# Tiles 61 and 62 stored each in its own transfer instead of together: the last stores of a matmul with bias and residual

## The chip, the cores and the metric

One core of one Trainium2 chip. The metric is the device time of one execution in microseconds (us), as a median of several. Engines: PE is TensorE, DVE is VectorE, ACT is ScalarE, POOL is GpSimd, SP is the engine that issues all transfers. "The 16 engines" below are the core's DMA engines.

## The reference

```python
def setup_inputs():
    batch, m, k, n = 16, 512, 1024, 768      # x, weight, bias, residual, all float32
    ...
def reference(x, weight, bias, residual):
    return (np.matmul(x, weight) + bias + residual).astype(np.float32)
```

That is 8192 rows in 64 tiles of 128 rows by 768 columns. In and out together are 87 MB.

## The kernel before

Sixteen tiles make a group; in the output, 16 rows of one partition lie next to each other, so a store of several tiles is 128 rows of (tiles x 3072) bytes. SP issues loads ("x", "r", "w", "b") and stores ("s" for whole tiles, "c" for a column piece of the last one) strictly in the order of one list. An entry goes out when all that it needs is done:

```python
ORDER = [ ... cut ...
 ('r', 3, 7, 16), ('s', 2, 0, 16), ('s', 3, 0, 10), ('s', 3, 10, 13),
 ('s', 3, 13, 15), ('c', 3, 15, 0), ('c', 3, 15, 1)]
OUTSIDE = 4
LAST = [(0, 512), (512, 256)]

    def pump():
        while queue:
            kind, S, j0, j1, *cut = queue[0]
            ... cut ...
            else:
                need = [("out", J * S + j) for j in range(j0, j1)]
            if not all(n in done for n in need):
                return
            queue.pop(0)
```

So ('s', 3, 13, 15) stores tiles 61 and 62 once both are done. Tile 63 is computed and stored in two column pieces, of 512 and 256 columns. The end of the program waits for the landing of the stores: all but the last four, then a barrier, then the last four.

```python
    with tc.tile_critical():
        landed = prog.emit(stores)
        for sem, value in landed[:-OUTSIDE]:
            nc.sync.wait_ge(sem, value)
    with tc.tile_critical(sync_engine=mybir.EngineType.SP):
        for sem, value in reversed(landed[-OUTSIDE:]):
            nc.sync.wait_ge(sem, value)
```

Of the kernel before, what the change touches and what calls it, by code (L numbers as in the profile page):

```python
# [32 lines left out]
 ('r', 1, 6, 16), ('s', 0, 0, 16), ('x', 2, 0, 6), ('r', 2, 0, 6), ('x', 2, 6, 16),  # L33
 ('r', 2, 6, 16), ('s', 1, 0, 16), ('x', 3, 0, 6), ('r', 3, 0, 7), ('x', 3, 6, 16),
 ('r', 3, 7, 16), ('s', 2, 0, 16), ('s', 3, 0, 10), ('s', 3, 10, 13),
 ('s', 3, 13, 15), ('c', 3, 15, 0), ('c', 3, 15, 1)]
OUTSIDE = 4
LAST = [(0, 512), (512, 256)]

# [368 lines left out]
```

## Time and profile before

| | before |
|---|---|
| time, median of 3 runs | 210.03 us (209.96 to 210.3) |
| span of the profiled run | 208.5 us |
| TensorE busy | 97% |
| DMA engines busy on the main queue | 97.9% |
| result of tile 61 / of tile 62 there | 200.53 / 202.61 us |
| last result there | 204.60 us |
| last piece landed | 207.27 us |

The lines are in the prediction. Three views matter: the timeline of the end (when a result is there), the issues with their time to landing (when a store is complete), and the half-microsecond stretches, whose second last column is the mean busy share of the 16 DMA engines. A share of 0.5 does not say whether each engine is half busy or half of them are idle. The records of single increments and packets in the trace do: each store raises its semaphore 16 times, once for each DMA engine. Times told below as "first increment" and "last increment" are from these records, as are packet times.

Two more stretches of before, which the result will be held against (start and end, then busy time of PE, PEld, DVE, ACT, POOL, the granted clock, the DMA share, GB/s):

```profile
204.50:205.00 0.50, 0.00 (x0) 0.00 (x0) 0.10 (x1) 0.00 (x0) 0.00 (x0) 1.00 0.99 393
206.00:206.50 0.50, 0.00 (x0) 0.00 (x0) 0.00 (x0) 0.00 (x0) 0.00 (x0) 1.00 0.90 318
```

Most engines are busy until 206.5; then only the last one still works (its last packet ends at 206.93).

### The profile page before, as it was taken

Reading aid. Unit: us, or ns where it says so; the run is one execution under the profiler, and the core shown is the slowest. Engines: PE = TensorE matmul, PEld = TensorE weight load, DVE = VectorE, ACT = ScalarE, POOL = GpSimd, SP = SyncE. Lnnn points to the kernel's source line nnn. Section 1 sums busy time; section 2 is a strip of 40 time slices with the busy share of each in tenths; the row PEclk is TensorE's granted clock in tenths of the full one; section 3 lists DMA queues with packets and bytes.
Section 4 is the critical chain, followed back from the end, with each engine's and each line's share of the span. In section 5 each row is a group of like instructions: output and inputs, shape, how many; then the busy total and the mean of one; then the engine's idle time right before and its main releaser. Section 6 shows DMA issues by size and latency. Waiting matters only on the chain.

```text
span 208.5 us, 2492 instructions
## 1 busy us (share of the span) xinstructions
PE 201.6 (97%) x1298; PEld 80.8 (39%) x794; DVE 105.3 (51%) x141; ACT 66.1 (32%) x69; POOL 115.2 (55%) x71
## 2 busy tenths in 40 slices
PE   7899999999999999999999999999999999999991
PEld 2333434443443444344334434433443443344340
DVE  1457555445545543654554454555445545544542
ACT  2444522402640282420280094230092047430000
POOL 1100029859999904999029801999207960899200
PEclk9999999999999999999999999999999999999998
DMA  5999999899999999999998999999999999999985
GB/s 216 425 425 445 426 423 475 385 427 425 485 409 416 449 395 438 453 396 437 410 493 387 432 445 429 443 443 385 423 450 468 416 398 471 415 443 417 427 351 232
DMA packets 4627, 87.20 MB, mean 418 GB/s; under 512 B 516, under 2 KB 644, under 8 KB 1416
## 3 DMA queue, kind: packets, MB, share of 16 engines
q1 hardware_dynamic: 4616, 87.05, 97.9%
q8 instruction: 8, 0.13, 0.2%
q14 instruction: 3, 0.02, 0.0%
HBM read 61.88 MB, written 25.17 MB: 417 GB/s over the span
## 4 chain that ended last, share of the span: by engine, by line
PE 92%; DMA 4%; DVE 1%; SPq 0%; ACT 0%; issue 0%
PE psum_o L257 79%; PE pt L250 13%; DMA x_tile<-in_x_dram 4%; SPq L168 0%; DVE xt L226 0%; ACT xb L226 0%; DVE ro L229 0%; SPq L403 0%; SPq L371 0%
## 5 line engine op out<-in xcount | busy, mean ns | idle before, releaser
L257 PE MATMUL psum_o<-w_sb,xt 128*128 128x256 bf16 (+1 forms) x1024 | 176.6, 326 | 0.5 <-DVE xt L226 0.5
L229 POOL TENSOR_TENSOR ro<-ro,bias_sb 128x768 f32<-128x768 f32 x50 | 88.8, 1817 | 46.9 <-DMA ro<-in_residual_dram 46.9
L226 ACT CAST xb<-x_tile 128x1024 bf16<-128x1024 f32 (+1 forms) x63 | 61.3, 1023 | 117.1 <-DMA x_tile<-in_x_dram 88.6
L268 PEld LDWEIGHTS <-xt 128*128 128x128 bf16 x520 | 50.9, 98 | 102.9 <-issue 101.0
L226 DVE COPY xt<-pt 128x1024 bf16<-128x1024 bf16 x64 | 44.1, 691 | 83.4 <-PE pt L250 83.4
L229 DVE TENSOR_TENSOR ro<-psum_o,ro 128x768 f32<-128x768 f32 (+2 forms) x51 | 47.6, 934 | 6.5 <-POOL ro L229 4.5
L250 PE MATMUL pt<-ident,xb 128*128 128x128 f32 x256 | 38.3, 274 | 0.6 <-DVE xb L226 0.4
L229 POOL TENSOR_TENSOR ro<-ro 128x768 f32<-128x768 f32 x14 | 24.9, 1818 | 25.0 <-DMA ro<-in_residual_dram 24.9
L250 PEld LDWEIGHTS pt<-ident,xb 128*128 128x128 f32 x256 | 29.7, 141 | 15.6 <-issue 12.3
L229 DVE TENSOR_TENSOR ro<-psum_o,bias_sb 128x768 f32<-128x768 f32 x14 | 13.2, 948 | 0.0
L312 PE MATMUL psum_o<-warm 128*128 128x512 bf16 x18 | 6.3, 506 | 1.4 <-DVE warm_a L232 1.4
L226 DVE CAST xb<-x_tile 128x512 bf16<-128x512 f32 (+1 forms) x4 | 1.9, 492 | 6.2 <-DMA x_tile<-in_x_dram 6.2
L226 ACT CAST w_sb<-ro 128x768 bf16<-128x768 f32 x4 | 3.3, 832 | 3.7 <-DMA ro<-in_weight_dram 3.7
L226 POOL CAST w_sb<-ro 128x768 bf16<-128x768 f32 x1 | 0.8, 822 | 6.0 <-DMA ro<-in_weight_dram 6.0
L312 PEld LDWEIGHTS psum_o<-warm 128*128 128x128 bf16 x18 | 2.1, 124 | 4.5 <-issue 2.7
L226 DVE CAST w_sb<-ro 128x768 bf16<-128x768 f32 x3 | 1.7, 557 | 2.0 <-DMA ro<-in_weight_dram 2.0
L226 ACT ACT_TABLE_LOAD x1 | 1.3, 1283 | 0.9 <-SPq L371 0.9
L329 DVE STREAM_SHUFFLE bias_sb<-bias_row 128x768 f32<-128x768 f32 x1 | 1.0, 1007 | 0.0
L232 DVE MEMSET warm<- 128x256 uint32 x1 | 0.3, 272 | 1.1 <-SPq L371 1.1
L232 DVE MEMSET bias_row<- 128x768 f32 x1 | 0.7, 698 | 0.2 <-issue 0.2
L232 POOL MEMSET ident<- 128x128 f32 x1 | 0.2, 204 | 0.5 <-SPq L371 0.5
L320 POOL TENSOR_SCALAR_AFFINE_SELECT ident<-ident 128x128 f32<-128x128 f32 x1 | 0.3, 292 | 0.2 <-POOL ident L232 0.2
(7 smaller groups left out, 0.7 us busy)
## 6 DMA issues: line engine op xcount, KB each, us to landing
out_dram<-ro SPq DMA_DIRECT2D x3, 6144.0 KB, 34.6
x_tile<-in_x_dram SPq DMA_DIRECT2D x3, 5120.0 KB, 24.5
ro<-in_residual_dram SPq DMA_DIRECT2D x3, 3840.0 KB, 32.4
x_tile<-in_x_dram SPq DMA_DIRECT2D x3, 3072.0 KB, 34.0
ro<-in_residual_dram SPq DMA_DIRECT2D x3, 2304.0 KB, 18.7
x_tile<-in_x_dram SPq DMA_DIRECT2D x4, 1024.0 KB, 10.9
x_tile<-in_x_dram SPq DMA_DIRECT2D x2, 2048.0 KB, 23.4
out_dram<-ro SPq DMA_DIRECT2D x1, 3840.0 KB, 13.3
```

Of the source, the lines that this page charges most:

```text
L226: op(eng, lambda e: (e.copy if eng == "act" else e.tensor_copy)(out=dst, in_=src), rd, wr)
L229: op(eng, lambda e: e.tensor_add(out=dst, in0=a, in1=b), rd, wr)
L232: op(eng, lambda e: e.memset(dst, v), [], [wr])
L250: op("pe", lambda e, q=q: e.transpose(out=pt[:, q, :], in_=words[:, ts(q, P)], identity=ident), [("XB", t % XB_N, 2 * q // n_q), "ident"], ...
L257: return e.add_instruction(mybir.InstMatmult(name=nc.get_next_instruction_name(), ins=[e.lower_ap(rhs), e.lower_ap(lhsT, for_matmul_weight ...
L268: op("pe", lambda g: g.ldweights(lhsT), rd)
L312: op("pe", lambda e: e.matmul(PO[i][:, 0:512], lhsT=warm[:, 0:P], rhs=warm, start=True, stop=True), ["warm"], [("PO", i)])
L320: op("pool", lambda e: e.affine_select(out=ident, in_=ident, compare_op=mybir.AluOpType.not_equal, fill=1.0, base=0, pattern=[[-1, P]], ch ...
L329: op("dve", lambda e: e.stream_shuffle(out=bias_sb, in_=bias_row, mask=[0] * QUAD), ["bias_row"], ["bias"])
```

## The change

The intent: tile 61 is done two microseconds before tile 62 and need not wait for it.

```diff
- ('s', 3, 13, 15), ('c', 3, 15, 0), ('c', 3, 15, 1)]
+ ('s', 3, 13, 14), ('s', 3, 14, 15), ('c', 3, 15, 0), ('c', 3, 15, 1)]
```

OUTSIDE stays 4, so the store of tiles 58 to 60 is now waited for ahead of the barrier.

## The prediction

> **What bounds the kernel now.** I read the page first (busy shares, slices, chain), then the timeline and the waits of the last ten microseconds, because the change touches only one of the last stores.
>
> The page, parts 1, 2 and 4:
> ```profile
> span 208.5 us, 2492 instructions
> PE 201.6 (97%) x1298; PEld 80.8 (39%) x794; DVE 105.3 (51%) x141; ACT 66.1 (32%) x69; POOL 115.2 (55%) x71
> ...
> DMA  5999999899999999999998999999999999999985
> ...
> q1 hardware_dynamic: 4616, 87.05, 97.9%
> ...
> PE 92%; DMA 4%; DVE 1%; SPq 0%; ACT 0%; issue 0%
> ```
> Two things run flat out side by side: TensorE, busy 97% of the span, and the DMA engines, 97.9% of 16 engines' time on one queue. No stage up to the last few microseconds is touched, so all that can be won or lost lies after the last matmul, and in how far the stores are behind it there. The timeline of the end, columns start, duration, engine and instruction, with the idle time before it in brackets:
> ```profile
> 196.55 0.95 DVE L229 TENSOR_TENSOR ro<-psum_o,ro 128x768 f32<-128x768 f32 x1
> 199.58 0.95 DVE L229 TENSOR_TENSOR ro<-psum_o,ro 128x768 f32<-128x768 f32 x1
> 201.65 0.96 DVE L229 TENSOR_TENSOR ro<-psum_o,ro 128x768 f32<-128x768 f32 x1 [1.11 <-PE psum_o L257]
> 203.30 0.69 DVE L229 TENSOR_TENSOR ro<-psum_o,ro 128x512 f32<-128x512 f32 x1 [0.70 <-PE psum_o L257]
> 204.18 0.42 DVE L229 TENSOR_TENSOR ro<-psum_o,ro 128x256 f32<-128x256 f32 x1 [0.18 <-PE psum_o L257]
> ```
> These are the results of tiles 60, 61 and 62 and the two column pieces of tile 63. Tile 61 is complete at 199.58 + 0.95 = 200.53, but its store goes with tile 62 and leaves only at 201.65 + 0.96 = 202.61. The last result is there at 204.60, 3.9 us before the span ends. What SP waits for from 204 us on, and the issues of the last stores with their time to landing (one line each for tiles 58 to 60, for 61 with 62, and for the last piece):
> ```profile
> SPq L403 <- DMA out_dram<-ro: 1.4, 3, 0.6
> ```
> ```profile
> out_dram<-ro SPq DMA_DIRECT2D x1, 1152.0 KB, 6.9
> out_dram<-ro SPq DMA_DIRECT2D x1, 768.0 KB, 3.7
> out_dram<-ro SPq DMA_DIRECT2D x1, 128.0 KB, 2.6
> ```
> The landings follow: 197.52 + 6.9 = 204.4; 202.63 + 3.7 = 206.3; 204.63 + 2.6 = 207.2. So the kernel ends with the landing of the last 128 KB at about 207.3 and 1.2 us of closing barriers. The question is whether that landing is late because its data came late or because the DMA engines still had older stores to move. Stretches of half a microsecond (columns: engines' busy time, then granted clock, DMA share, GB/s):
> ```profile
> 201.50:202.00 0.50, 0.50 (x4) 0.20 (x2) 0.35 (x1) 0.00 (x0) 0.00 (x0) 1.00 0.92 387
> 202.00:202.50 0.50, 0.50 (x4) 0.24 (x3) 0.50 (x1) 0.00 (x0) 0.00 (x0) 1.00 0.74 313
> 202.50:203.00 0.50, 0.50 (x4) 0.25 (x3) 0.10 (x1) 0.00 (x0) 0.00 (x0) 1.00 0.61 258
> 203.00:203.50 0.50, 0.50 (x6) 0.36 (x4) 0.20 (x1) 0.00 (x0) 0.00 (x0) 1.00 0.53 221
> 203.50:204.00 0.50, 0.50 (x6) 0.32 (x4) 0.49 (x1) 0.00 (x0) 0.00 (x0) 1.00 0.96 399
> ```
> The dip from 202.0 to 203.5 is real idle time, and it is what the change aims at. It adds up to (0.26 + 0.39 + 0.47) x 0.5 = 0.56 us of all 16 engines, but it is a mean: about half of them stand still, and the others do not. The trace's packet records and the increments of each store's semaphore, one per engine, show which. The 16 increments for tiles 58 to 60 come at 202.13, 202.25, 202.36, 202.47, 203.04, 203.05, 203.44, then 203.76 to 204.19, and the last at 204.44; a packet ends about 0.35 us before its increment, so the engines run out of older work between 201.8 and 204.09. The packets of tiles 61 and 62 begin at 203.47, 0.84 us after their issue. The last engine has no gap: its 9216-byte packets end at 204.08, its eight 6144-byte ones at 205.93, its eight of 2048 at 206.58, its eight of 1024 at 206.93, and its increment is the last one, at 207.27. For every store after 200 us the last increment is 0.24 to 0.30 us behind the fifteenth. The end is the end of this one engine's work.
>
> **What the Trainium skill says.** "Perfetto Trace Analysis", DMA Optimizations, says that splitting may let some chunks start sooner, and helps if DMA engines are generally idle; here they are 97.9% busy and only partly idle for 1.5 us. "DMA: Bandwidth & Descriptors", Queues, rings and completion order: on each engine descriptors are consumed in ring order. The trace agrees: an engine's packets for tile 61 stand behind its own for 58 to 60, whatever time they are issued. The same page, "Why a DMA increments its semaphore by 16 and not by 1": only the full count means that all has landed, so the slowest engine decides; the 16 separate increments above agree. The same page, Bandwidth, advises transfers of 1 MiB and more; here packets cost, by size, 46 ns (1024 B), 84 (2048), 121 (3072, the bias load), 234 (6144) and 347 (9216), some 8 ns plus 0.037 ns a byte, so halving a 768 KB store costs little.
>
> **The change part by part.** Instruction order on TensorE, VectorE, ScalarE and GpSimd is the same; only SP's list changes.
> 1. Removed: one store of 128 rows of 6144 B, issued at 202.63. Added: one of tile 61, 128 rows of 3072 B, issued at about 200.54, and one of tile 62, the same size, still at 202.63. Tile 61's 384 KB become available to the engines 2.09 us earlier.
> 2. SP: one more issue of about 0.33 us (the five stores' issues take 332 to 344 ns each). It falls at 200.54 to 200.87, when SP would be waiting for tile 62. Off the path: 0.
> 3. Engines: each moves 8 packets of 3072 B twice in place of 8 of 6144. Per engine 16 x 121 - 8 x 234 = 1936 - 1872 = +64 ns, and one more semaphore write of 9 ns: +0.07 us.
> 4. Engines that are early (about ten: increments up to 203.83, so packets done by about 203.5): tile 61's packets fill their gap. With first packets possible at 200.54 + 0.84 = 201.4, an engine free at 201.8 does them until 202.8, waits for tile 62 at 203.47, ends it at 204.45, and then waits for the two pieces of tile 63 (204.02 and 204.63 plus 0.84 = 204.86 and 205.47): ends near 205.9 instead of 206.5. That is a gain of 0.6 us for it, and worth nothing for the count of 16.
> 5. The last engine: 204.08 + 16 x 0.121 + 0.01 = 206.03 instead of 205.93; the last piece ends at 206.93 + 0.07 to 0.10 = about 207.0. No gap to fill, so no gain; loss 0.07 to 0.10 us.
> 6. The waits at the end: the program waits for the last four stores after a barrier and for the others before it. With one store more, the store of tiles 58 to 60 is no longer among the last four and moves to the waits before the barrier. It lands at 204.44; SP reaches these waits at 205.0. One more check there, some 0.05 us, is hidden, as SP then waits for stores until 207.3 anyway.
> Sum: +0.07 us on the path, of which I take back 0.05 because with these ten engines done earlier the last may run its packets slightly faster. 210.03 + 0.02 = 210.05.
>
> **The rivals.**
> First: the gap is filled and the end comes earlier. For it: the dip in the DMA share, tile 61 waiting 2.1 us for nothing, and 3.9 us of tail after the last result. The most it could give: the last piece, issued at 204.63, would on free engines need 0.84 + 0.37 + 0.35 = 1.56 us and land at 206.2, so about 1.0 us; limited by the one tile that is moved, 8 x 0.121 = 0.97. Against it: the gap must be on the last engine, and there is none. If in other executions the last engine is less late, so that it too waits for 203.47, part of it could come: perhaps 209.5.
> Second: the shorter packets and the extra store cost more than their fit, for example a gap between stores on each engine of 0.1 to 0.2 us. Against it: in the records an engine goes from 6144-byte to 2048-byte packets with some 10 ns between. It would make 210.2.
> Third: the earlier writes of tile 61 get in the way of the older store on the late engines, or move which engine is last. Reordering among engines can shift the last by the 0.24 to 0.30 us between fifteenth and sixteenth, either way: 209.8 to 210.3.
>
> **Range and chances.** The three runs before spread over 0.34 us (209.96 to 210.3), more than my net effect. Runs on another chip can add as much again. I put the time at 210.05, eight times in ten between 209.5 and 210.5; the lower end holds half of the first rival's 1.0 us. A change of 2% is 4.2 us; the whole tail after the last result is 3.9 us and the moved tile is worth 0.97, so faster by 2% is out of reach (0.004), and nothing added comes near 4.2 us (0.006). Within 2%: 0.99.
>
> **What would show it.** Right: the DMA share from 201.5 to 203.5 rises to near full; a 384 KB store issued near 200.5; SP waits at the end as long as before (1.4 us in three pieces, a few hundredths apart); the last increment again near 207.3, with the early engines' increments for the last piece now down to about 206.3, so a wider spread among the 16; packets of 3072 B at 121 ns. Wrong: last increment by 206.8 or earlier with the span down to 208.0, which would mean that the last engine's lateness is not its own backlog, or 3072-byte writes well over 121 ns.

## The result

| | before | the change |
|---|---|---|
| median, 6 runs each | 210.00 us (209.96 to 210.38) | 210.18 us (210.09 to 210.35) |
| ratio | | 1.0005, 95% interval 0.9992 to 1.0017 |

A ratio is the mean time of one kernel's runs over that of the other's of the same rounds, so not quite the ratio of the medians. The same, within what can be resolved (0.12% of 210 us is 0.25 us).

The page of the changed kernel, the parts that were shown of before:

```profile
span 208.4 us, 2468 instructions
PE 200.3 (96%) x1273; PEld 80.9 (39%) x794; DVE 105.3 (51%) x141; ACT 66.1 (32%) x69; POOL 115.2 (55%) x71
...
DMA  6999999999999999999999999999999999999995
...
q1 hardware_dynamic: 4760, 87.05, 97.9%
...
PE 92%; DMA 4%; issue 1%; DVE 1%; SPq 0%; ACT 0%
```

The span is the same and the same chain bounds it. The 25 missing PE instructions are matmul records missing from the trace (the main matmul's group counts 999 where before has 1024), not work saved. The queue has 144 packets more: 128 more of data, and 16 semaphore writes for one more store.

The timeline of the end (VectorE), the issues with their landing, and SP's waits after 204 us:

```profile
199.79 0.95 DVE L229 TENSOR_TENSOR ro<-psum_o,ro 128x768 f32<-128x768 f32 x1
201.85 0.96 DVE L229 TENSOR_TENSOR ro<-psum_o,ro 128x768 f32<-128x768 f32 x1 [1.11 <-PE psum_o L257]
```
```profile
out_dram<-ro SPq DMA_DIRECT2D x1, 1152.0 KB, 6.6
out_dram<-ro SPq DMA_DIRECT2D x1, 384.0 KB, 4.5
out_dram<-ro SPq DMA_DIRECT2D x1, 128.0 KB, 2.4
```
```profile
SPq L403 <- DMA out_dram<-ro: 1.1, 3, 0.6
```

In this profiled run all results came 0.2 us later than in that of before (tile 61 at 200.74 in place of 200.53). Tile 61's store of 384 KB did leave at once, at 200.76, and landed at 205.28. The last piece was issued at 204.83 in place of 204.63, yet it landed at 207.20, where before has 207.27. That is why SP waits 1.1 us in place of 1.4: it comes later, and what it waits for comes at the same time. A landing that does not follow its issue has something else ahead of it.

The stretches, the five of before and the two added above:

```profile
201.50:202.00 0.50, 0.50 (x4) 0.27 (x3) 0.15 (x1) 0.00 (x0) 0.00 (x0) 1.00 0.97 406
202.00:202.50 0.50, 0.50 (x4) 0.25 (x3) 0.50 (x1) 0.00 (x0) 0.00 (x0) 1.00 1.02 424
202.50:203.00 0.50, 0.50 (x4) 0.24 (x3) 0.31 (x1) 0.00 (x0) 0.00 (x0) 1.00 0.79 332
203.00:203.50 0.50, 0.50 (x5) 0.28 (x3) 0.00 (x0) 0.00 (x0) 0.00 (x0) 1.00 0.62 252
203.50:204.00 0.50, 0.50 (x7) 0.44 (x6) 0.42 (x1) 0.00 (x0) 0.00 (x0) 1.00 0.92 369
...
204.50:205.00 0.50, 0.00 (x0) 0.00 (x0) 0.30 (x1) 0.00 (x0) 0.00 (x0) 1.00 0.68 270
206.00:206.50 0.50, 0.00 (x0) 0.00 (x0) 0.00 (x0) 0.00 (x0) 0.00 (x0) 1.00 0.55 193
```

The gap that the change aimed at is partly filled: 0.97 and 1.02 from 201.5 to 202.5, where before has 0.92 and 0.74 (1.02 is not more than all: the share adds up recorded durations, and neighbouring records overlap a little, see experiment 7). But what was taken there comes back as new idle time: 0.68 from 204.5 (before: 0.99) and 0.55 from 206.0 (before: 0.90). Most engines are now ahead and wait for the pieces of tile 63, and at the very end for one another. The increments of the last piece say it in numbers: the middle one of the 16 came at 206.83 before and at 206.58 now; the last one at 207.27 and 207.20. The many gained 0.25 us, the one that counts nothing that can be told from chance.

### The profile page after: what moved, and what is told of

The parts are those of the page before. It is cut to its first block, busy times and chain, and to the rows that moved or that the text cites. A ratio compares the mean times of both kernels' runs of the same rounds, so it can differ in the third digit from the quotient of the medians.

```text
span 208.4 us, 2468 instructions
## 1 busy us (share of the span) xinstructions
PE 200.3 (96%) x1273; PEld 80.9 (39%) x794; DVE 105.3 (51%) x141; ACT 66.1 (32%) x69; POOL 115.2 (55%) x71
## 4 chain that ended last, share of the span: by engine, by line
PE 92%; DMA 4%; issue 1%; DVE 1%; SPq 0%; ACT 0%
PE psum_o L257 79%; PE pt L250 13%; DMA x_tile<-in_x_dram 4%; SPq L168 0%; DVE xt L226 0%; ACT xb L226 0%; DVE ro L229 0%; SPq L403 0%; SPq L371 0%
```

## The experiments

Theory A, from the prediction: the end is the end of the last DMA engine's work. That engine has no gap, so a tile offered to it earlier waits behind its older packets. Rivals: C, the last piece's own way from issue to landing sets the end; D, idle time of the engines counts as its mean; E, the moved wait costs something.

**1. The change again.** No edit; the same kernel once more, with the repeat of run 2 and with run 3.

> The change itself once more, on the same chip as the next two runs, so that they can be compared. Theory A: +0.0 to +0.1 us against the kernel before; ratio 1.000 within 0.001.

Measured: 210.06 us (209.93 to 210.33, 5 runs), before 210.05 us (11 runs); ratio 1.0001 (0.9989 to 1.0013). As theory A expects. Two occasions now agree on "no difference above some 0.3 us".

**2. Is the moved wait a cost?** Five waits after the barrier put the store of tiles 58 to 60 back where it was.

```diff
- OUTSIDE = 4
+ OUTSIDE = 5
```

> The change with the store of tiles 58 to 60 put back among the waits after the barrier (five in place of four). Theory A: that wait is hidden either way, so the same as the change within 0.05 us (210.1), last increment and span unchanged. If the moved wait cost the change something, this is up to 0.1 us faster than the change.

Measured: 209.98 us (4 runs), before 210.21 us (10 runs); ratio 0.9989 (0.9975 to 1.0003). That was lower than expected, and the interval just reaches 1, so it was repeated in one call with the change and with run 3:

> The change with five waits after the barrier, once more. The first time it was 0.23 us under the kernel before, 0.3 us under what the change showed on another occasion. Theory A (the moved wait is hidden, the difference was chance in how late the last DMA engine is): same as the change of this call within 0.1 us. Rival E (the moved wait costs): 0.2 to 0.3 us faster than the change again.

Measured: 210.15 us (209.8 to 210.5, 5 runs); ratio 1.0007 (0.9994 to 1.0019), now 0.09 us slower than the change. The first result did not come again. The trace of the change agrees: SP is through the waits ahead of the barrier at 205.31, and the last piece lands at 207.20.

**3. The moved wait alone**, on the kernel before:

```diff
- OUTSIDE = 4
+ OUTSIDE = 3
```

> The kernel before with three waits in place of four after the barrier: the moved wait alone, without splitting the store. Theory A: the same as before within 0.1 us. Rival E: +0.2 to +0.3 us.

Measured: 210.2 us (6 runs, 209.96 to 210.24 but for one of 211.53); ratio 1.0013 (0.9994 to 1.0033). The interval alone would leave room for rival E; it is widened by the one odd run, without which the mean is 210.13. Rival E asked for 0.2 to 0.3 us; neither the repeat of run 2 nor this run shows it. A cost of less than some 0.2 us would not be seen.

These runs also give the plainest evidence for theory A. Last increments in us, each from one profiled run:

| run | tiles 58 to 60 | last piece | difference |
|---|---|---|---|
| before | 204.44 | 207.27 | 2.83 |
| before, three waits | 204.47 | 207.22 | 2.75 |
| the change | 204.38 | 207.20 | 2.82 |
| the change again | 204.11 | 206.91 | 2.80 |
| the change, five waits | 204.10 | 206.89 | 2.79 |
| the same again | 203.93 | 206.76 | 2.83 |

Joint or split, the last piece lands 2.75 to 2.83 us after the last engine is through with tiles 58 to 60. That moment itself wanders by half a microsecond from run to run, and it is set before the store in question moves a byte: the last increment of the store of tiles 48 to 57, which is alike in all six, came at 201.69, 201.72, 201.64, 201.38, 201.37 and 201.19 in the same order. The last packet of that store ended at 201.33 at the latest, and the first packet of a split tile 61 began at 201.61 at the earliest. The last engine is not always alone: at the last piece the sixteenth increment is 0.30 and 0.29 us behind the fifteenth in before and in the change, but only 0.00 to 0.06 in the other four runs, where at least two engines share the end.

**4. No backlog: the change where it can help.** Tiles 58 to 60 are not stored at all (a wrong result), so that no engine has older work when tile 61 is done. First with tiles 61 and 62 together:

```diff
- ('s', 3, 0, 10), ('s', 3, 10, 13), ('s', 3, 13, 15),
+ ('s', 3, 0, 10), ('s', 3, 13, 15),
```

> Wrong result on purpose: tiles 58 to 60 are never stored, so no engine has older work when tile 62 is ready; tiles 61 and 62 stored together. Theory A: all engines start them at 203.47, end the last piece at 206.4, last increment 206.75 in place of 207.27: -0.5 us against the kernel before. Serves as the base of the next run. Rival C: 0.

Then with the two apart:

```diff
- ('s', 3, 0, 10), ('s', 3, 10, 13), ('s', 3, 13, 15),
+ ('s', 3, 0, 10), ('s', 3, 13, 14), ('s', 3, 14, 15),
```

> Wrong result on purpose, as the run before it, with tiles 61 and 62 stored singly: the change under test without backlog. Theory A: tile 61 goes from 201.4, tile 62 from 203.47 to 204.45, the pieces of 63 end at 205.9, last increment near 206.25: -0.5 us against the joint form without backlog, -1.0 against the kernel before. If the change does nothing by nature (rival C, the last piece's own way decides): no difference between the two.

Measured: together 209.95 us (209.87 to 210.08, 5 runs), ratio to before 0.9985 (0.9972 to 0.9999); apart 209.44 us (209.41 to 209.96, 5 runs), ratio 0.9964 (0.995 to 0.9978). The same edit that gives nothing in the kernel gives 0.51 us here. The stretches, together and then apart:

```profile
202.00:202.50 0.50, 0.50 (x4) 0.25 (x3) 0.50 (x1) 0.00 (x0) 0.00 (x0) 1.00 0.00 0
202.50:203.00 0.50, 0.50 (x4) 0.20 (x2) 0.25 (x1) 0.00 (x0) 0.00 (x0) 1.00 0.00 0
203.00:203.50 0.50, 0.50 (x5) 0.32 (x4) 0.05 (x1) 0.00 (x0) 0.00 (x0) 1.00 0.00 0
```
```profile
202.00:202.50 0.50, 0.50 (x5) 0.20 (x3) 0.38 (x1) 0.00 (x0) 0.00 (x0) 1.00 1.03 412
202.50:203.00 0.50, 0.50 (x4) 0.26 (x3) 0.50 (x1) 0.00 (x0) 0.00 (x0) 1.00 0.66 258
203.00:203.50 0.50, 0.50 (x4) 0.22 (x3) 0.07 (x1) 0.00 (x0) 0.00 (x0) 1.00 0.00 0
```

Here a share of 0.00 does mean that all 16 engines stand still, and tile 61's packets fill the hole. Two things were off. Against before, the joint form gained 0.26 us in place of 0.5, and the split form 0.77 in place of 1.0; experiment 6 tells why. The difference of the two came out as expected because both fell short by the same quarter of a microsecond. And the profiled run of the split form was its slowest (209.96; the other four lie between 209.41 and 209.60): its last piece was issued at 205.10, 0.32 later than in the joint run's profile, and landed at 206.94, 1.84 us after its issue. With the backlog gone, the end followed the last result in that run, so that a late result was a late end.

**5. Tile 61 taken off the engines.** The change without its new store (a wrong result):

```diff
- ('s', 3, 13, 14), ('s', 3, 14, 15),
+ ('s', 3, 14, 15),
```

> Wrong result on purpose: the change with tile 61 never stored, so its 0.97 us are gone from every engine. Theory A: the last engine ends 0.97 us earlier, held to about 0.85 by the waits for tile 63's pieces: -0.85 us against the kernel before, last increment near 206.4. Rival C: 0.

Measured: 209.46 us (209.37 to 209.56, 5 runs), before 210.21; ratio 0.9963 (0.9951 to 0.9976), 0.75 us less where 0.85 was expected. The last piece:

```profile
out_dram<-ro SPq DMA_DIRECT2D x1, 128.0 KB, 1.8
```

1.8 us from issue to landing, where before has 2.6. It is the same 128 KB, issued in the same way; only the older work on the engines is less. Rival C falls: the piece's own way takes 1.8 us, and what before has above that is the queue ahead of it.

**6. The opposite step, and steps between.** Fewer, larger stores at the end. Tiles 58 to 62 in one:

```diff
- ('s', 3, 10, 13), ('s', 3, 13, 15),
+ ('s', 3, 10, 15),
```

> The opposite step: tiles 58 to 62 in one store, ready only with tile 62 (about 202.6 us, first packets 203.5). Theory A, the last DMA engine's backlog sets the end: that engine finishes the store of tiles 48 to 57 at about 201.3, now stands idle until 203.5, and the end moves by this, +2.1 us (about 212.1 us, 1% slower), last increment of the last piece near 209.4. Rival C, the end is set by the last piece's own way from issue to landing: 0. Rival D, any idle engine time counts as its mean over the 16: mean idle about 2.8 us in place of 0.56, so +2.3 us, hardly told from A here.

Measured: 212.68 us (4 runs), before 210.24; ratio 1.0115 (1.010 to 1.013), 2.44 us more. The stretches in the wait for tile 62:

```profile
199.50:200.00 0.50, 0.50 (x5) 0.17 (x2) 0.50 (x2) 0.00 (x0) 0.00 (x0) 1.00 0.43 184
...
201.00:201.50 0.50, 0.50 (x5) 0.20 (x3) 0.00 (x0) 0.00 (x0) 0.00 (x0) 1.00 0.00 0
...
203.00:203.50 0.50, 0.50 (x6) 0.39 (x4) 0.24 (x1) 0.00 (x0) 0.00 (x0) 1.00 0.72 307
```

Now the last engine too has a gap, and the end pays for it. So waiting to store is far from free in this kernel; it is free only as long as the last engine does not run dry.

Tiles 58 and 59, then 60 to 62:

```diff
- ('s', 3, 10, 13), ('s', 3, 13, 15),
+ ('s', 3, 10, 12), ('s', 3, 12, 15),
```

> Stores of tiles 58 and 59, then 60 to 62. Theory A: the last engine ends tiles 58 and 59 at about 201.34 + 8 x 0.235 = 203.25, waits 0.25 us for tile 62's store, then runs three tiles (2.78 us): +0.35 us with what 0.1 us of packet rounding adds (210.35 us), last increment near 207.6. Rival C: 0. Rival D: mean idle about 0.9 in place of 0.56 us, +0.35, not told from A.

Measured: 210.85 us (5 runs), ratio 1.0032 (1.0019 to 1.0044): +0.61 where 0.35 was expected.

Tiles 58 to 61, then 62:

```diff
- ('s', 3, 10, 13), ('s', 3, 13, 15),
+ ('s', 3, 10, 14), ('s', 3, 14, 15),
```

> Stores of tiles 58 to 61, then 62 alone. The first is ready at 200.5, first packets 201.4, which is when the last engine ends the store before it (201.34), while the early engines have stood idle since 199.1. Theory A: 0 (-0.1 to +0.1 us). Rival D (mean idle counts): mean idle before 201.4 is about 0.75 us in place of 0.56, +0.2 us. Rival C: 0.

Measured: 210.78 us (5 runs), ratio 1.0027 (1.0014 to 1.0039): +0.54 where 0 was expected. This is a miss of theory A as it was put: the expected gap of the last engine was 0.05 us.

All three, and the joint run of experiment 4, are slower than expected by a quarter of a microsecond or more (0.24 to 0.54), and the records say where that quarter is. When a store is queued behind another, the last engine of before takes (204.44 - 201.69) / 3 = 0.917 us a tile, from increment to increment. When a store finds all engines idle, its landing should be: first packet, plus 0.917 us a tile, plus the 0.35 us from packet to increment.

| store that finds all engines idle | first packet | worked out | landed | excess |
|---|---|---|---|---|
| 58 to 62 (five tiles) | 203.42 | 208.36 | 208.62 | 0.26 |
| 60 to 62 (three) | 203.50 | 206.60 | 206.85 | 0.25 |
| 58 to 61 (four) | 201.58 | 205.60 | 205.86 | 0.26 |
| no backlog, 61 and 62 (two) | 203.61 | 205.79 | 206.08 | 0.29 |
| no backlog, 61 (one) | 201.87 | 203.14 | 203.38 | 0.24 |

The excess does not grow with size: it is a price of starting from idle, 0.24 to 0.29 us. About half of it is that the 16 engines' first packets do not begin together (their starts spread over 0.12 to 0.15 us in these five); for the rest, packets running side by side were a little longer (9216 bytes: 355.9 ns on average in the 60 to 62 store, 347.5 in before). How the rest divides stays open. With this term the misses close: tiles 60 to 62 had 0.35 + 0.25 = 0.60 expected, 0.61 measured; for 58 to 61, the first packet began at 201.58. In before, the last engine's packets of the store ahead end at 201.33 and it goes on at once, so the gap is 0.25 and not 0.05, and 0.25 + 0.26 = 0.51 of the 0.54 is told. In before and in the change the last engine never starts from idle.

**7. The packet cost made large.** All fifteen tiles from 48 to 62 stored singly:

```diff
- ('s', 3, 0, 10), ('s', 3, 10, 13), ('s', 3, 13, 15),
+ ('s', 3, 0, 1), ('s', 3, 1, 2), ... one for each tile ... ('s', 3, 14, 15),
```

> All fifteen tiles 48 to 62 stored singly: the packet cost made large. Theory A: per engine 15 x 8 x 0.121 = 14.52 us of packets in place of 9.10 + 2.78 + 1.87 = 13.75, so +0.77 us, and 12 more semaphore writes of 0.009 to 0.03 us: +0.9 to +1.1 us (about 211.0 us). The rival that earlier stores are a gain: the time falls. Rival C: 0.

Measured: 210.92 us (210.54 to 210.94, 5 runs), ratio 1.0026 (1.0014 to 1.0039): slower, +0.55 to 0.68 us by ratio or medians, where 0.9 to 1.1 was expected. Earlier stores are no gain where engines are busy; the sign is theory A's, the size is not. The last increments come every 0.945 us, so 118.1 ns a packet with its share of a semaphore write. For the ten-tile store of before it is (201.69 - 192.60) / 8 = 1136 ns for 30720 bytes, 113.6 for 3072. So 4.5 ns for each packet, semaphore included, where the recorded durations had suggested 8: the records of one engine's packets overlap by 3 to 4 ns (3072-byte packets of 121 ns begin 117.6 ns apart on the last engine), and durations added up count that twice. The tiles of the three-tile and two-tile stores had cost 114.6 and 115 ns for 3072 bytes, so the sum is 80 x 4.5 + 24 x 3.5 + 16 x 3.1 = 494 ns, close under what was measured.

No version here beats both kernels by more than chance: what shortened the end (experiments 4 and 5) left out work.

## Why the prediction was right

- **The bound and the gap.** Right. The last engine had no gap; experiments 1, 4 and 5 show the three sides of it: no gain with the backlog, 0.51 us without, 0.75 us when work is taken off. The last increments at a constant distance behind tiles 58 to 60 show the same. "This one engine" was too narrow: in four of the six runs of the table at least two engines end together.
- **Steps 1 and 2** (tile 61 leaves two microseconds earlier, one more issue off the path). Right: issued 200.76, 332 ns long. One small thing was not foreseen: the first piece of tile 63 now leaves 1.46 us after tile 62's store, 1.39 before, while the second leaves 2.00 us after it in both. The cause is not known; it is off the path, as the engines are still at tile 62 by then (its last increment: 206.23).
- **Steps 3 and 5** (0.07 to 0.10 us more on the last engine). Right in sign, too large: from the landing of tiles 58 to 60 to that of tile 62 the last engine took 1.85 us in the change and 1.84 in before. Experiment 7 puts a packet's cost at 4.5 ns, so 8 more packets are 0.04 us. The 0.05 us that was taken back made up for this, for another reason than the one given (the last engine running faster beside fewer others), which no run tested by itself. That the net came out near +0.02 is luck, and the runs could not tell +0.02 from 0.
- **Step 4** (early engines gain, for nothing). Right: the first increment of the last piece was expected near 206.3; it came at 206.50 in the profiled run with late results and at 206.30 in the change run again. The middle one moved from 206.83 to 206.58 and 206.51.
- **Step 6** (the moved wait is hidden). Right: experiments 2 and 3.
- **What would show it.** Two signs of "right" failed. The DMA share was to rise to near full up to 203.5; it did so only up to 202.5, as the early engines finish tile 61 by then and wait for tile 62, which step 4 itself had said. And SP's wait was to stay within hundredths of 1.4 us; it was 1.1, as the results of that run came 0.2 us later against an unmoved landing. And a sign of "wrong" did appear: in the repeat with five waits the last increment came at 206.76 with a span of 208.0. It does not mean what the prediction had it mean, because in that run the end of tiles 58 to 60 was early by as much (203.93), and the distance was 2.83 as in before. A fixed time was a poor sign, as the end wanders by half a microsecond; the distance was the one to name.
- **The rivals.** The first (gap filled, end earlier) falls for this kernel and is right for one without backlog. D, its refined form, falls with the result itself: the middle increment gained 0.25 us and the end did not follow (0.25 us would be a ratio of 0.9988, and the interval begins at 0.9992). The second (shorter packets) is 0.04 us. The third (which engine is last, and by how much) is no effect of the change but is the run-to-run scatter: last increments from 206.76 to 207.27.

What stays open is an effect under some 0.2 us: ratios of 1.0005 and 1.0001 with intervals of 0.12% either way cannot show +0.02 us. It is open, too, why engines are behind, though the records point to the program's own instruction fetches. In the profiled run of before all 16 increments of each large load come within 0.5 us up to 23.15 us; at 23.84 an instruction packet of 16384 bytes takes 1.10 us on one engine, and at the next landing (29.96) one increment is 1.31 us behind the fifteenth. Eight such packets and three of 8192 bytes fall in the span. Count the increments that come more than 0.7 us behind the first of their transfer: 0 up to 23.15, 1 after that packet, 2 after the one at 47.38, 3 after 60.37, 4 after 71.48, 5 after 95.67, 7 after two at 112.0 and 115.08, 8 after 120.48, and 12 after the last, at 194.62. The change run again goes through the same counts. That each packet puts one more engine behind is the plain reading; but the records do not name the engine and no run moved these packets, so it is argued and not shown.

## What to carry to other kernels

Before splitting a store to send a part earlier, ask whether the last DMA engine has a gap there, not whether the mean DMA share dips: a dip of 0.56 us was worth nothing that could be told from chance, because the gap was on the engines that were ahead. Measure the landing against the landing of the store ahead of it; if that distance stays, the work on the engine sets the end, and here only leaving out bytes brought it forward. In the other direction there is a cliff: a store held back until all engines are idle cost its gap and a quarter of a microsecond of starting up.

## What the Trainium skill lacked or had wrong

- "DMA: Bandwidth & Descriptors", Bandwidth, advises batches of 1 MiB and more for 75% of the peak; its figures are of loads issued from GpSimd. For stores issued from SP and queued one behind another the advice does not hold: the singly stored tiles of 384 KB landed 0.945 us apart on the last engine, 416 GB/s; the 1152 KB store took 2.75 us there, 429 GB/s. The difference is 3%.
- The same page, Why small descriptors are slow, gives a fixed overhead of about 3 cycles a packet and 32 bytes a cycle, and speaks of small descriptors only. It held at 3072 bytes too, and was a better source than the recorded durations: with the 850 MHz that its Bandwidth section names, 3072 bytes come out as (96 + 3) / 0.85 = 116 ns (an estimate), and 118.1 with the semaphore's share was measured, where the record's duration is 121.
- The same page, Latency and other measured facts, has about 600 ns to the first byte for transfers issued as here. Where engines were idle, 0.83 us was measured from the start of the issue to the first packet, of which the issue is 0.33.
- No page has the price of a store that finds all engines idle against one queued behind another: 0.24 to 0.29 us, whatever its size from 384 to 1920 KB.
- "Perfetto Trace Analysis", DMA Optimizations, ties splitting to engines that are "generally idle". What decides is the last engine: with a mean share of 0.53 to 0.74 for 1.5 us the split gave nothing (ratio 1.0005 and 1.0001), with all engines idle it gave 0.51 us.
